# The opening of an attention stage: constant rows filled by GpSimd, and the first head's loads issued from GpSimd's queue

## The chip, the cores and the metric

The kernel runs on one core of a Trainium2 chip. A core has five engines that work in parallel, each through its own list of instructions in order: TensorE (matmuls, PE in the profile), VectorE (DVE), ScalarE (ACT), GpSimd (POOL) and SyncE (SP), which here only issues DMAs. The metric is the time of one execution on the device, in microseconds; lower is better. The time before is the median of three runs, 2979.34 us (2972.79 to 2981.46).

## What is computed

One layer of a hybrid encoder over 2064 positions (16 meta tokens and 2048 inputs) of width 1024. An input projection feeds three groups of heads side by side: an RG-LRU recurrence, a forgetting attention with 8 heads of 64, and an RWKV-7 recurrence. Their outputs go through one output projection, and a gated feed-forward block follows. The attention, cut to its core:

```python
qh = heads(q) * (HEAD_DIM ** -0.5)
kh, vh = heads(k), heads(v)
c = jnp.cumsum(log_sigmoid(f_logit + f_bias), axis=1)     # per head
s = jnp.einsum('bhqd,bhkd->bhqk', qb, kh) + (cb[..., :, None] - c[..., None, :])
s = jnp.where(kpos[None, :] <= qpos[:, None], s, -jnp.inf)
p = jax.nn.softmax(s, axis=-1)
o = jnp.einsum('bhqk,bhkd->bhqd', p, vh)
```

So each score is a product of a query and a key plus a difference of two cumulated gates.

## The kernel before, in words

The program has stages. First the input projection, in three parts over the positions, which writes queries, keys and values to scratch in HBM: `scr["qh"]` and `scr["ql"]` hold a query's high and low part, `kh` and `kl` those of a key, `ch` and `cl` those of the cumulated gate. Beside it run the two recurrences, block by block; their last blocks are still under way when the attention begins. Then come the attention, the output projection, and the feed-forward block in two halves.

The attention (class `Attn`) goes over two halves; in each it goes over the 8 heads, and per head over two steps `b` of 512 queries. In the first half a head has 1040 keys (`KHALF`), in the second 2064. A step has two parts. `maxima` computes the scores of a step once, in pieces into `mx` (L581), and reduces each to a row maximum on VectorE (L586). `weights` computes the scores again, transposed, into `sc` (L710 with `k1` and `q1`, L711 with `k2` and `q2`), takes the exponential on ScalarE and multiplies by the values into `po` (L733). The maxima run up to two steps ahead of the weights (`AHEAD`), so three sets of query tiles are in a ring.

The sums need constant rows. Of each tile, the partitions 0 to 63 hold data and the partitions 64 to 127 hold constants or rows that are added to the product:

- `q3` (queries for the maxima, three of them): zeros, then ones in two rows. `fixed` writes them with three memsets on VectorE, over 64 partitions (L496), three (L497) and one (L498), of 512 columns each.
- `q2` (queries for the second product, three of them): zeros, one memset on VectorE (L478). Row 64 is written later, with the negated maximum.
- `k2` (keys, two tiles in the first half): row 64 is one, the rest zero, written by four VectorE copies of a broadcast column of the identity (L504) of 520 columns each. Rows 65 and 66 are then overwritten by loads of `ch` and `cl` (L544, L545). Each tile holds two heads: heads 0 and 1 use the first, heads 2 and 3 the second.

`k1` holds the key's high and low part and has no constants. `keys` issues a head's five loads (L542 to L547), `maxima` the four loads of a step's queries (L568 to L571): `q3`, `q1` twice, `q2`. All are issued from SyncE, in the same list as the recurrences' small loads and stores (L1236 among them).

The order of instructions on each engine isn't the order of the source. A planner goes through the whole program with its own estimates and lists an instruction once what it needs is there, so instructions of the recurrences and of the attention stand mixed in the lists of all engines, up to about 1090 us. Attention's tiles lie on memory of the input projection, and the first of its instructions stand in each list behind the input projection's last ones.

GpSimd's work in the attention is the causal mask at the diagonal (L717), most of the sums of weights (L754) and part of the divisions. Before it, it does small steps of the recurrences (L1222, L1233, L1244). DMAs from its queue occur at two places, the zero columns at the program's start (L2204) and the last attention step's division (L781 to L804).

Of the kernel before, what the change touches and what calls it, by code (L numbers as in the profile page):

```python
# [8 lines left out]
F32 = mybir.dt.float32  # L9
# [23 lines left out]
class Core:  # L33


    def __init__(self, tc, ctx):
        self.tc = tc
        self.nc = tc.nc
        self.ctx = ctx
        self.uid = 0  # L40
        nc = self.nc
        self.const = ctx.enter_context(tc.tile_pool(name="const", bufs=1))
        self.ident = self.const.tile([P, P], F32, name="ident")
        make_identity(nc, self.ident[:])
        self.flip = 0
        self.root = self.apart = False
        self.turns = 0
# [319 lines left out]
KHALF = META + 8 * P  # L367
# [85 lines left out]
class Attn:  # L453
# [7 lines left out]
    def __init__(self, core, pool, psum, more, scr):  # L461
        self.core, self.pool, self.psum, self.more, self.scr = core, pool, psum, more, scr
        self.wide, self.bank, self.place, self.tail = False, 0, 0, False
        nc = self.nc = core.nc
        self.clock, self.later, self.serial, self.added = 0, [], 0, 0
        self.pending, self.loads, self.steps, self.beside = None, [], [], iter(())
        self.marks = {}
        self.place_p = 0


        self.turn = {"k": 1, "k2": 1, "q2": 0, "q3": 0}
        self.ring = {s: [] for s in self.turn}
        for i in range(self.AHEAD + 1):
            q3 = pool.tile([P, 512], F32R, tag=f"q3_{i}", name=core.n("q3"), bufs=1)
            self.fixed(q3, None, self.ONES)
            self.ring["q3"].append(q3)
            q2 = pool.tile([P, 512], F32R, tag=f"q2_{i}", name=core.n("q2"), bufs=1)
            nc.vector.memset(q2[64:128].bitcast(F32), 0.0)  # L478
            self.ring["q2"].append(q2)
            if i > 1:  # L480
                continue
            k1 = pool.tile([P, 2, KHALF], F32R, tag=f"k1_{i}", name=core.n("k1"), bufs=1)
            self.rear(pool, f"k2_{i}")
            v1 = pool.tile([P, 2, NKT // 2 + 1, 64], F32, tag=f"v1_{i}", name=core.n("v1"), bufs=1)
            self.ring["k"].append((k1, v1))

    def rear(self, pool, tag):
        k2 = pool.tile([P, 2, KHALF], F32R, tag=tag, name=self.core.n("k2"), bufs=1)
        self.fixed(None, k2, self.ONES)
        self.ring["k2"].append(k2)  # L490

    def fixed(self, q, k, ones):

        if q is not None:

            self.nc.vector.memset(q[64:128].bitcast(F32), 0.0)  # L496
            self.nc.vector.memset(q[64 : 64 + ones + 2].bitcast(F32), 1.0)  # L497
            self.nc.vector.memset(q[64 : 64 + ones].bitcast(F32), 0.0)  # L498
        if k is not None:
            if ones == 1:  # L500
                col = self.core.ident[64:128, 64:65]
                kf = k.rearrange("p h t -> p (h t)")
                for c in range(0, 2 * KHALF, KHALF // 2):
                    self.nc.vector.tensor_copy(kf[64:128, c : c + KHALF // 2], col.to_broadcast([64, KHALF // 2]))  # L504
            else:
                self.nc.gpsimd.memset(k[64:128].bitcast(F32), 0.0)
                self.nc.gpsimd.memset(k[64 : 64 + ones].bitcast(F32), 1.0)
# [18 lines left out]
    def keys(self, h, nt):  # L526

        nc, scr = self.nc, self.scr
        n = META + P * (nt - 1)
        r = slice(64 * h, 64 * h + 64)  # L530
        if n <= KHALF:

            i, half = divmod(self.place, 2)
            self.place = (self.place + 1) % 4
            k1, v1 = (t[:, half] for t in self.ring["k"][i])
            k2 = self.ring["k2"][i][:, half]
        else:
            (k1, v1), k2 = self.next("k"), self.next("k2")
            k1, k2 = (t[:].rearrange("p h t -> p (h t)") for t in (k1, k2))
            v1 = v1[:].rearrange("p h j d -> p (h j) d")  # L540
        k1f, k2f = k1.bitcast(F32), k2.bitcast(F32)
        nc.sync.dma_start(k2f[0:64, :n], scr["kh"][r, :n])  # L542
        g = 64 + self.ONES
        nc.sync.dma_start(k2f[g : g + 1, :n], scr["ch"][h : h + 1, :n])  # L544
        nc.sync.dma_start(k2f[g + 1 : g + 2, :n], scr["cl"][h : h + 1, :n])  # L545
        nc.sync.dma_start(k1f[0:64, :n], scr["kh"][r, :n])
        nc.sync.dma_start(k1f[64:128, :n], scr["kl"][r, :n])  # L547

        def values():
            nc.sync.dma_start(v1[:, : nt - 1], scr["v"][: n - META, r].rearrange("(j p) d -> p j d", p=P))  # L550
            nc.sync.dma_start(v1[:META, nt - 1], scr["v"][n - META : n, r])


        self.loads.append(values)
        return k1, k2, v1

    def maxima(self, h, b, keys):

        nc, core, scr = self.nc, self.core, self.scr
        k1, k2, v1 = keys  # L560
        r = slice(64 * h, 64 * h + 64)
        t0, n, ref = META + 512 * b, 512, 4 * b
        qt = [(P * i, P, META + P * (4 * b + i)) for i in range(4)]
        ts = slice(t0, t0 + n)
        q3 = self.next("q3")
        q1 = self.t([P, 512], "q1", F32R, self.AHEAD + 1)
        q2 = self.next("q2")
        nc.sync.dma_start(q3[0:64, :n].bitcast(F32), scr["qh"][r, ts])  # L568
        nc.sync.dma_start(q1[0:64, :n].bitcast(F32), scr["qh"][r, ts])
        nc.sync.dma_start(q1[64:128, :n].bitcast(F32), scr["qh"][r, ts])  # L570
        nc.sync.dma_start(q2[0:64, :n].bitcast(F32), scr["ql"][r, ts])  # L571
        nq = len(qt)
        mc = self.t([P, 4, 5], "mc")
        nc.vector.memset(mc[:], NEG)
        for i, (qo, rows, prior) in enumerate(qt):
            for ci in range(len(MAX_CUTS) - 1):
                a, e = MAX_CUTS[ci], min(MAX_CUTS[ci + 1], prior + rows)
                if a >= e:
                    break
                ps, last = self.mx(), e == prior + rows  # L580
                nc.tensor.matmul(ps[:rows, : e - a], q3[:, qo : qo + rows], k2[:, a:e], start=True, stop=not last)  # L581
                if last:
                    nc.tensor.matmul(
                        ps[:rows, prior - a : e - a], core.identb[:], core.futureb[:], start=False, stop=True
                    )
                self.reduced = nc.vector.tensor_reduce(  # L586
                    mc[:rows, i, ci : ci + 1], ps[:rows, : e - a], axis=AX.X, op=ALU.max
                )
                yield None
        bias = self.t([P, NKT], "bias", bufs=self.AHEAD + 1)  # L590
        yield q1, q2, bias
        sh = self.t([P, 4], "sh")
        nc.vector.tensor_reduce(sh[:], mc[:], axis=AX.X, op=ALU.max)
        ps = self.mx()
        for i in range(nq):
            nc.tensor.transpose(ps[0:1, P * i : P * i + P], sh[:, i : i + 1], core.ident[:])
        nc.scalar.activation(q2[64:65], ps[0:1], AF.Identity, scale=-1.0, bias=core.ncref[:, ref, h : h + 1])
        nc.scalar.activation(
            bias[:], core.ccol[:, :, h], AF.Identity, scale=-1.0, bias=core.cref[:, ref, h : h + 1]
        )  # L600
        yield None
# [70 lines left out]
    def pieces(b):  # L672

        ends = [META + P * (4 * b + i + 1) for i in range(4)]
        return sum(sum(a < e for a in MAX_CUTS[:-1]) for e in ends)

    def weights(self, h, b, keys, queries, fill):


# [1766 lines left out]
```

## Time and profile before

| | |
|---|---|
| median of three runs | 2979.34 us |
| the profiled execution, its own time | 2974.88 us |
| span of the profile, first to last instruction | 2973.2 us |
| mean granted TensorE clock | 0.980 |
| first attention load issued by SyncE (L542) | 869.60 us |
| first attention matmul (L710) | 877.62 us |
| last transposed scores (L711) | 1515.5 us |
| DMA share of GpSimd's queue (q0) | 0.93 MB of 530.52 MB |

A row of the profile gives line, engine, operation, the tile written and the tiles read, and the number of instructions; buffer numbers are left out of the names, so `q1`, `q2` and `q3` all appear as `q`, `k1` and `k2` as `k`. Arrows in brackets name what ended an engine's wait. The granted clock is the share of TensorE's full rate that the chip allowed in a stretch.

### The profile page before, as it was taken

How to read it: one execution, taken by the hardware profiler on the slowest of the kernel's cores; microseconds unless marked ns; L12 is line 12 of the kernel's file. 1: busy time of each engine (PE TensorE's matmuls, PEld its weight loads, DVE VectorE, ACT ScalarE, POOL GpSimd, SP SyncE). 2: the span in 40 equal slices, each digit the busy share in tenths (PEclk: the TensorE clock that was granted, in tenths of full speed). 3: DMA queues.
4: the chain of work that ended last, by engine and by line, in shares of the span. 5: the costliest groups of instructions: out<-in, count | busy, mean ns of one | idle time of the engine just before them, and what ended most of it. 6: DMA issues, size and time to landing. Idle time of an engine off the chain costs nothing.

```text
span 2973.2 us, 53343 instructions
## 1 busy us (share of the span) xinstructions
PE 2840.2 (96%) x18854; PEld 2448.6 (82%) x18854; DVE 2015.4 (68%) x3974; ACT 1505.3 (51%) x2937; POOL 1281.3 (43%) x1555
## 2 busy tenths in 40 slices
PE   6999999999978889999999999999999999999998
PEld 6998899889865555566568999999999999787887
DVE  5257654675678766556756988888778787646766
ACT  4246432444346555445635665666575665324333
POOL 1001121131214566766722667455655444656443
PEclk9999899999989899999999999999999999999999
DMA  6776479576654257535245665577777774436453
GB/s 219 235 233 223 156 246 322 171 240 213 209 127 95 70 130 215 125 95 130 72 133 187 204 191 173 167 230 211 205 212 219 218 199 131 155 114 222 148 171 121
DMA packets 470344, 530.52 MB, mean 178 GB/s; under 512 B 86862, under 2 KB 356888, under 8 KB 468524
## 3 DMA queue, kind: packets, MB, share of 16 engines
q1 hardware_dynamic: 469308, 526.18, 58.4%
q8 instruction: 148, 2.42, 0.3%
q14 instruction: 120, 0.98, 0.1%
q0 software_dynamic: 768, 0.93, 0.1%
HBM read 368.07 MB, written 158.90 MB: 177 GB/s over the span
## 4 chain that ended last, share of the span: by engine, by line
PE 72%; DVE 8%; DMA 7%; ACT 5%; POOL 4%; issue 3%; SPq 1%; DVEq 0%; POOLq 0%; ACTq 0%
PE psu L181 9%; PE psu L182 9%; PE psu L183 9%; PE psp L183 5%; PE psp L182 5%; PE psp L181 5%; PE psd L181 4%; PE psd L182 4%; PE psd L183 4%; PE po L733 3%; PE sc L710 2%; PE pswo L181 2%; PE pswo L182 2%; PE pswo L183 2%; PE mx L581 2%
## 5 line engine op out<-in xcount | busy, mean ns | idle before, releaser
L182 PE MATMUL psu<-xo,uw 128*128 128x344 f32 x1848 | 591.5, 320 | 0.0
L181 PE MATMUL psu<-xo,uw 128*128 128x344 f32 x1848 | 586.0, 322 | 3.5 <-DVE vb L1907 2.1
L183 PE MATMUL psu<-xo,uw 128*128 128x344 f32 x1848 | 581.9, 320 | 0.3 <-DVE uw L1716 0.3
L181 PE MATMUL psp<-xh,wh 128*128 128x384 f32 (+2 forms) x1152 | 378.3, 328 | 0.1
L183 PE MATMUL psp<-xh,wl 128*128 128x384 f32 (+2 forms) x1152 | 377.0, 328 | 0.7 <-DMA wl<-scr_wk 0.7
L182 PE MATMUL psp<-xl,wh 128*128 128x384 f32 (+2 forms) x1152 | 377.6, 328 | 0.0
L1716 DVE TENSOR_TENSOR uw<-uq,uw 128x512 fp32r<-128x512 f32 x341 | 318.8, 940 | 61.3 <-ACT uw L1715 58.3
L181 PEld LDWEIGHTS psu<-xo,uw 128*128 128x128 f32 x1848 | 345.8, 188 | 5.1 <-DVE vb L1907 3.1
L182 PEld LDWEIGHTS psu<-xo,uw 128*128 128x128 f32 x1848 | 347.2, 188 | 0.0
L183 PEld LDWEIGHTS psu<-xo,uw 128*128 128x128 f32 x1848 | 345.7, 188 | 1.1 <-DVE uw L1716 1.1
L1715 ACT ACTIVATE uw<-uq 128x512 fp32r<-128x512 f32 x462 | 288.1, 627 | 100.1 <-PE psu L183 47.3
L715 ACT ACTIVATE p<-sc,bias 128x512 f32<-128x512 f32 (+4 forms) x352 | 196.4, 590 | 166.8 <-PE sc L711 141.9
L586 DVE TENSOR_REDUCE mc<-mx 128x1 f32<-128x512 f32 (+5 forms) x352 | 191.8, 566 | 119.4 <-PE mx L581 82.9
L1855 DVE SCALAR_TENSOR_TENSOR uy<-psu,ffn_cols,uy 128x342 f32<-128x342 f32 (+1 forms) x390 | 220.6, 567 | 62.4 <-ACT uy L1853 60.7
L1716 POOL TENSOR_TENSOR uw<-uq,uw 128x512 fp32r<-128x512 f32 x121 | 184.1, 1521 | 136.7 <-ACT uw L1715 112.9
L1863 POOL TENSOR_TENSOR uy<-uy,uy 128x342 f32<-128x342 f32 (+1 forms) x132 | 144.2, 1092 | 228.7 <-DVE uy L1855 63.1
L183 PEld LDWEIGHTS psp<-xh,wl 128*128 128x128 f32 x1152 | 219.9, 191 | 7.1 <-issue 4.6
L181 PEld LDWEIGHTS psp<-xh,wh 128*128 128x128 f32 x1152 | 219.8, 191 | 4.5 <-issue 2.6
L182 PEld LDWEIGHTS psp<-xl,wh 128*128 128x128 f32 x1152 | 220.0, 191 | 3.7 <-issue 2.3
L754 POOL TENSOR_TENSOR acc<-acc,p 128x512 f32<-128x512 f32 (+3 forms) x186 | 196.5, 1059 | 48.5 <-DVE acc L754 21.4
L1716 DVE TENSOR_TENSOR fo<-u,fo 128x896 fp32r<-128x896 f32 x88 | 100.3, 1140 | 133.0 <-ACT fo L1715 132.4
L1715 ACT ACTIVATE fo<-u 128x896 fp32r<-128x896 f32 x88 | 81.2, 923 | 207.6 <-PE psd L183 122.3
(489 smaller groups left out, 6301.5 us busy)
## 6 DMA issues: line engine op xcount, KB each, us to landing
uq<-scr_us SPq DMA_DIRECT2D x220, 256.0 KB
uq<-in_ffn_up_dram SPq DMA_DIRECT2D x209, 256.0 KB
wl<-scr_wk SPq DMA_DIRECT2D x48, 512.0 KB
wh<-scr_wk SPq DMA_DIRECT2D x48, 512.0 KB
u<-scr_ff SPq DMA_DIRECT2D x88, 256.0 KB
scr_ff<-uy SPq DMA_DIRECT2D x110, 171.0 KB
raw<-in_w_in_dram SPq DMA_DIRECT2D x24, 512.0 KB
scr_wk<-wh SPq DMA_DIRECT2D x24, 512.0 KB
```

The source lines that it names most:

```text
L181: nc.tensor.matmul(out, ah, bh, start=first, stop=False, skip_group_check=more)
L182: nc.tensor.matmul(out, ah, bl, start=False, stop=False, skip_group_check=more)
L183: nc.tensor.matmul(out, al, bh, start=False, stop=last, skip_group_check=more)
L581: nc.tensor.matmul(ps[:rows, : e - a], q3[:, qo : qo + rows], k2[:, a:e], start=True, stop=not last)
L586: self.reduced = nc.vector.tensor_reduce(mc[:rows, i, ci : ci + 1], ps[:rows, : e - a], axis=AX.X, op=ALU.max)
L715: last = nc.scalar.activation(p[:rows, :w], ps[:rows, :w], AF.Exp, bias=bias[:rows, j : j + 1])
L733: mm = nc.tensor.matmul(po[at : at + 64, c0:n], v1[:rows, j], p[:rows, : n - c0], start=start and i < 2, stop=end and i + 2 >= len(group), ...
L754: eng.tensor_tensor(a, ps_[0][0][:rows, c0:n] if start and i == 1 else a, p[:rows, : n - c0], op=ALU.add)
L1715: core.nc.scalar.activation(hi, src, AF.Copy)
L1716: (eng or core.nc.vector).tensor_tensor(lo, src, hi, op=ALU.subtract)
L1855: core.conved = stt(y[:, :n], src[:, i : n + i], cw[:, 44 * i + cc : 44 * i + cc + 1], y[:, :n], op0=ALU.mult, op1=ALU.add)
L1863: core.pooled = nc.gpsimd.tensor_tensor(v[:, :n], g[:, :n], v[:, :n], op=ALU.mult)
```

## The change

Three edits. The constants of the six query tiles are written by memsets on GpSimd. The second key tile's constants are written by two GpSimd memsets over all its 2080 columns, 64 partitions and then one, in place of four VectorE copies; the first key tile stays on VectorE. And for the first head in the first half, the loads of `k2` (three) and the query loads of its two steps (eight) are issued from GpSimd instead of SyncE; the two loads of `k1` stay on SyncE.

```diff
         for i in range(self.AHEAD + 1):
             q3 = pool.tile([P, 512], F32R, tag=f"q3_{i}", name=core.n("q3"), bufs=1)
-            self.fixed(q3, None, self.ONES)
+            self.fixed(q3, None, self.ONES, nc.gpsimd)
...
-            nc.vector.memset(q2[64:128].bitcast(F32), 0.0)
+            nc.gpsimd.memset(q2[64:128].bitcast(F32), 0.0)
...
-            self.rear(pool, f"k2_{i}")
+            self.rear(pool, f"k2_{i}", nc.gpsimd if i else None)
...
-    def fixed(self, q, k, ones):
+    def fixed(self, q, k, ones, eng=None):
         if q is not None:
-            self.nc.vector.memset(q[64:128].bitcast(F32), 0.0)
-            self.nc.vector.memset(q[64 : 64 + ones + 2].bitcast(F32), 1.0)
-            self.nc.vector.memset(q[64 : 64 + ones].bitcast(F32), 0.0)
+            eng = eng or self.nc.vector
+            eng.memset(q[64:128].bitcast(F32), 0.0)
+            eng.memset(q[64 : 64 + ones + 2].bitcast(F32), 1.0)
+            eng.memset(q[64 : 64 + ones].bitcast(F32), 0.0)
         if k is not None:
-            if ones == 1:
+            if ones == 1 and eng is None:
...
-        nc.sync.dma_start(k2f[0:64, :n], scr["kh"][r, :n])
+        queue = nc.gpsimd if h == 0 and n <= KHALF else nc.sync
+        queue.dma_start(k2f[0:64, :n], scr["kh"][r, :n])
         g = 64 + self.ONES
-        nc.sync.dma_start(k2f[g : g + 1, :n], scr["ch"][h : h + 1, :n])
-        nc.sync.dma_start(k2f[g + 1 : g + 2, :n], scr["cl"][h : h + 1, :n])
+        queue.dma_start(k2f[g : g + 1, :n], scr["ch"][h : h + 1, :n])
+        queue.dma_start(k2f[g + 1 : g + 2, :n], scr["cl"][h : h + 1, :n])
...
-        nc.sync.dma_start(q3[0:64, :n].bitcast(F32), scr["qh"][r, ts])
-        nc.sync.dma_start(q1[0:64, :n].bitcast(F32), scr["qh"][r, ts])
-        nc.sync.dma_start(q1[64:128, :n].bitcast(F32), scr["qh"][r, ts])
-        nc.sync.dma_start(q2[0:64, :n].bitcast(F32), scr["ql"][r, ts])
+        queue = nc.gpsimd if h == 0 and b < 2 else nc.sync
+        queue.dma_start(q3[0:64, :n].bitcast(F32), scr["qh"][r, ts])
+        queue.dma_start(q1[0:64, :n].bitcast(F32), scr["qh"][r, ts])
+        queue.dma_start(q1[64:128, :n].bitcast(F32), scr["qh"][r, ts])
+        queue.dma_start(q2[0:64, :n].bitcast(F32), scr["ql"][r, ts])
```

The other call of `fixed`, for the meta tokens in the second half, passes no engine and does what it did.

More of the change, by code (lines that the diff above doesn't have):

```diff
@@ L482, in __init__, with rear @@
             k1 = pool.tile([P, 2, KHALF], F32R, tag=f"k1_{i}", name=core.n("k1"), bufs=1)
-            self.rear(pool, f"k2_{i}")
+            self.rear(pool, f"k2_{i}", nc.gpsimd if i else None)
             v1 = pool.tile([P, 2, NKT // 2 + 1, 64], F32, tag=f"v1_{i}", name=core.n("v1"), bufs=1)
             self.ring["k"].append((k1, v1))
-    def rear(self, pool, tag):
+    def rear(self, pool, tag, eng=None):
         k2 = pool.tile([P, 2, KHALF], F32R, tag=tag, name=self.core.n("k2"), bufs=1)
-        self.fixed(None, k2, self.ONES)
+        self.fixed(None, k2, self.ONES, eng)
         self.ring["k2"].append(k2)
-    def fixed(self, q, k, ones):
+    def fixed(self, q, k, ones, eng=None):
         if q is not None:
-            self.nc.vector.memset(q[64:128].bitcast(F32), 0.0)
-            self.nc.vector.memset(q[64 : 64 + ones + 2].bitcast(F32), 1.0)
-            self.nc.vector.memset(q[64 : 64 + ones].bitcast(F32), 0.0)
+            eng = eng or self.nc.vector
+            eng.memset(q[64:128].bitcast(F32), 0.0)
+            eng.memset(q[64 : 64 + ones + 2].bitcast(F32), 1.0)
+            eng.memset(q[64 : 64 + ones].bitcast(F32), 0.0)
         if k is not None:
-            if ones == 1:
+            if ones == 1 and eng is None:
                 col = self.core.ident[64:128, 64:65]
```

## The prediction

> **What bounds the kernel now.** I read the page first: its busy times say that TensorE is the bound over the whole program. The change touches only the opening of the attention, so the whole-program shares say little; I went to the timelines of TensorE, VectorE, GpSimd and SyncE around 870 us, then to the table of stretches with the granted clock.
>
> ```profile
> PE 2840.2 (96%) x18854; PEld 2448.6 (82%) x18854; DVE 2015.4 (68%) x3974; ACT 1505.3 (51%) x2937; POOL 1281.3 (43%) x1555
> ```
> Columns of a timeline: start, length, engine, line, operation, and in brackets the idle time before it and what ended it. First TensorE at the seam between the input projection and the attention:
> ```profile
> 871.39 0.69 PE L1384 MATMUL rps<-rww,rwsc 128*64 128x64 f32 x16
> 877.62 1.10 PE L710 MATMUL sc<-q,k 128*128 128x512 f32 x2 [5.54 <-DMA q<-scr_qh]
> 883.73 0.49 PE L581 MATMUL mx<-k,q 128*128 128x144 f32 x1 [5.01 <-DVE q L498]
> ```
> The engine that is busy 96% of the program stands still here for 5.54 and 5.01 us, 10.5 us in all. The first gap ends with a load of queries, the second with a VectorE memset of a constant query row: just the two things that the change moves. This is what VectorE does meanwhile:
> ```profile
> 871.47 0.48 DVE L496 MEMSET q<- 64x512 f32 x1
> 872.51 1.46 DVE L504 CAST k<-ident 64x520 fp32r<-64x520 f32 x4
> 874.95 1.40 DVE L504 CAST k<-ident 64x520 fp32r<-64x520 f32 x4
> 877.97 0.42 DVE L1389 TENSOR_REDUCE rwgsm<-rps 128x4 f32<-128x256 f32 x1
> 883.19 1.03 DVE L498 MEMSET q<- 1x512 f32 x2 [0.16 <-DVE rwgsm L1390]
> ```
> It works without a pause: constants, and between them the recurrences' last block. GpSimd has nothing to do from 864.2 to 892.3 us, and SyncE gets to the attention's first load only at 869.6, behind the eight small loads of the recurrences:
> ```profile
> 863.88 0.31 POOL L1233 MEMSET rwxu<- 128x256 f32 x1 [4.69 <-PE rps L1328]
> 892.27 0.28 POOL L717 TENSOR_SCALAR_AFFINE_SELECT p<-p 128x112 f32<-128x112 f32 x1 [28.08 <-ACT p L715]
> 864.21 4.39 SPq L1236 DMA_DIRECT2D rwxu<-dx  x8
> 869.60 0.47 SPq L542 DMA_DIRECT2D k<-scr_kh  x1
> 873.31 0.26 SPq L544 DMA_DIRECT2D k<-scr_ch  x1
> 874.40 0.59 SPq L570 DMA_DIRECT2D q<-scr_qh  x1
> ```
> The clock makes the gap dearer than it looks (columns: stretch, its length, busy time of PE, PEld, DVE, ACT, POOL, granted clock, DMA share, GB/s):
> ```profile
> 875.00:876.00 1.00, 0.00 (x0) 0.00 (x0) 1.00 (x5) 0.00 (x0) 0.00 (x0) 1.00 0.74 176
> 876.00:877.00 1.00, 0.00 (x0) 0.00 (x0) 0.89 (x4) 0.00 (x0) 0.00 (x0) 0.52 0.73 207
> 884.00:890.00 6.00, 4.05 (x14) 2.28 (x14) 5.43 (x23) 1.45 (x3) 0.00 (x0) 0.50 1.20 221
> 890.00:900.00 10.00, 9.84 (x52) 7.48 (x52) 7.41 (x18) 4.50 (x11) 4.60 (x10) 0.67 1.06 216
> 896.00:897.00 1.00, 1.00 (x6) 0.52 (x6) 0.56 (x2) 0.65 (x3) 0.89 (x2) 0.74 1.06 216
> 897.00:898.00 1.00, 1.00 (x8) 0.70 (x7) 1.00 (x3) 0.54 (x4) 0.19 (x1) 1.00 1.00 200
> ```
> The clock falls to half at 876, about 3.9 us after TensorE's last matmul ended (872.1), and is whole again from about 896.4. From 884 to there TensorE is busy some 4.05 + 6.3 = 10.3 us at half rate; at the full rate the same matmuls would take about 5.2 us less.
>
> **The change, part by part.**
>
> *Off VectorE.* Twelve memsets (three query tiles, three for `q3` and one for `q2` each) and four of the eight casts, those of the second key tile:
> ```profile
> L496 DVE MEMSET q<- 64x512 f32 x3 | 1.5, 485 | 0.3
> L478 DVE MEMSET q<- 64x512 f32 x3 | 1.5, 485 | 0.2
> L497 DVE MEMSET q<- 3x512 f32 x3 | 1.5, 485 | 0.2 <-DVE rwrav L1134 0.2
> L498 DVE MEMSET q<- 1x512 f32 x3 | 1.5, 485 | 0.3 <-DVE rwgsm L1390 0.2
> ```
> 12 x 0.485 = 5.8 us plus 1.4 us of casts: 7.2 us. VectorE then holds only the first key tile's casts (871.5 to about 873), so the recurrences' L1389 can come near 873 instead of 878. That chain is not what TensorE waits for at the seam, so I book nothing for it alone.
>
> *Onto GpSimd.* The same twelve memsets, two memsets of 64x2080 in place of the four casts, and eleven issues of loads. The rows that price them lie far from here:
> ```profile
> 0.81 0.20 POOL masks.py:197 MEMSET ident<- 128x128 f32 x1 [0.29 <-POOLq L2432]
> 2.41 4.29 POOL L2204 DMA_DIRECT2D scr_p<-zeros  x8
> 9.55 1.60 POOL L2204 DMA_DIRECT2D scr_p<-zeros  x3 [2.86 <-DMA scr_p<-zeros]
> scr_p<-zeros POOLq DMA_DIRECT2D x12, 32.0 KB, 6.3
> rb<-scr_rden POOLq DMA_DIRECT2D x2, 128.0 KB, 2.9
> ```
> 128 columns take 0.20 us and 256 columns 0.31 (L1233 above): 0.11 us more for 128 columns, so 512 columns are some 0.53 us and 2080 some 1.9. This gives 12 x 0.53 = 6.4 us and 2 x 1.9 = 3.8 us. An issue is 4.29 / 8 = 0.54 us, eleven are 5.9 us. In all 16 us, in a hole of 28 us (864.2 to 892.3): the hole covers it, and without that cover it would stand in front of the first masks (L717). A load issued by GpSimd lands after 2.9 us where two of 128 KB are seen and after 6.3 us where twelve follow each other. I take 2.9, since the query loads are of that size and kind, and keep 6.3 for the range. The row with the 2.86 us shows the tenth of the twelve waiting for an earlier one of the same queue; should the ninth to eleventh here do so, only the second step's queries are late, and their matmuls come after those of the first step.
>
> *The waits that move.* The loads of the key tile's two rows `ch` and `cl` must still follow the VectorE casts. Today SyncE stands at L544 for them; afterwards GpSimd stands there instead, with the query loads behind it at worst. The casts end at about 872.9, before GpSimd has come that far by the sum below, so I price this at nothing; if GpSimd came early it would cost the difference, at most 872.9 less its arrival. SyncE keeps the `k1` loads and gets to the second head's keys up to 11 x 0.6 us earlier. The second key tile is first filled for the third head:
> ```profile
> 888.39 0.59 SPq L542 DMA_DIRECT2D k<-scr_kh  x1
> ```
> so its constants, done well before 880, are in time.
>
> *The sum.* The decisive chain is now GpSimd's. With memsets first, as they come in the program: 864.2 + 6.4 + 3.8 = 874.4; then the loads of `kh`, `ch`, `cl` and the first `q3`, 4 x 0.54 = 2.2, gives 876.6; landing 2.9 later, 879.5. The first matmul of the maxima moves from 883.7 to 879.5: 4.2 us earlier, and the first scores' `q1` (issued by 877.7, landed by 880.6) come about as late as that, so I take 4. TensorE still stands still for over 7 us, so the clock still falls and the 10 us at half rate stay. If the loads land in 6.3 us the gain is 0.8; if the planner lets the loads go ahead of the memsets of later tiles, the key rows bind: casts at 872.9, `ch` and `cl` issued by 874 and landed near 877, gain 6.7. Does it reach the end? In the stretch behind, TensorE is the fuller engine, and later there is no room at all:
> ```profile
> 1000.00:1200.00 200.00, 178.91 (x1167) 107.76 (x1166) 131.25 (x327) 108.87 (x220) 133.93 (x186) 0.93 0.57 148
> 1200.00:1400.00 200.00, 196.54 (x909) 128.70 (x909) 113.37 (x248) 101.11 (x185) 131.93 (x191) 1.00 0.44 110
> ```
> From 1200 us on TensorE is busy 196.54 of 200, so an earlier arrival there is an earlier end. Sum: 4 us off the span.
>
> *A rule that speaks against it.* The only copies on VectorE in GpSimd's new time are the four casts that stay, 1.46 us. The Trainium skill, page "SBUF — State Buffer", section on the two physical sides of the memory, warns that a VectorE copy in its two-port mode locks GpSimd out, so that it cannot write descriptors for its own DMAs. By that rule the casts hold GpSimd up by an estimated 1.5 us at most and the gain would be 2.5 us instead of 4; no row of this profile shows it either way, and the sum goes without it.
>
> *Against the runs.* The profiled execution took 2974.88 us, 1.7 more than its span of 2973.2, and lies 4.5 below the median of 2979.34, in runs that spread over 8.7 us. The sum makes 2974.88 into 2970.9; for a median I take the same 4 us off 2979.34 and predict 2975.
>
> **The rivals.**
>
> *More than the sum.* GpSimd's loads go ahead early, VectorE's part of the recurrences closes up too, and most of the 10.5 us of standing still goes; if what is left is shorter than the 3.9 us after which the clock fell, the 5.2 us of half rate go as well. That gives 9 to 16 us, 2963 to 2970. For it: both gaps are ended by moved work. Against it: the queue and the cast keep the keys incomplete until about 877.
>
> *It does not do what it says.* The planner placed the one-row memsets (L498) last on VectorE, long after the first ones; if it does so on GpSimd, with `ch` and `cl` behind them, 864.2 + 16 + 2.9 makes 883, as now. Time unchanged: 2979.
>
> *Slower.* Attention and the recurrences' last blocks are put in one order per engine by a planner, and a changed opening gives a new order up to about 1100 us. There TensorE already has holes that bring the clock down:
> ```profile
> 970.00:980.00 10.00, 6.92 (x30) 4.12 (x31) 8.77 (x27) 3.07 (x6) 4.40 (x8) 0.83 0.56 110
> 1110.00:1120.00 10.00, 6.40 (x32) 3.53 (x29) 8.20 (x19) 2.76 (x6) 6.97 (x12) 0.75 0.66 174
> ```
> One more such hole costs what the opening shows: 3.9 us of standing still and some 5.2 us of half rate, 9 us. One of them leaves 5 us more than before, which cannot be told from no change; from the second on it decides: 4 off, 18 on, 2993. For it: VectorE is the fuller engine in those rows. Against it: VectorE gets 7.2 us of room.
>
> A smaller one: the moved loads share the DMA engines with SyncE's, whose share is 1.06 to 1.20 from 884 on; they would land nearer 6.3 us. The Trainium skill, page "DMA: Bandwidth & Descriptors", section on issuing engines, says the same: other queues save only issue time. That is the 0.8 us end of the sum.
>
> **How the numbers follow.** The sum as worked out (gain of 1 to 8 us) 0.42; more than the sum 0.30; not doing what it says 0.13; slower 0.15. About 0.3%, 9 us, is what a measurement of this kernel can tell from no change. So faster by that is 0.30, within it 0.42 + 0.13 = 0.55, slower 0.15. The range goes from the far end of the first rival, 2963, to 2987, which takes in one more hole of the clock with the runs' own spread and leaves out most of the slower case. The likeliest case alone spans 2971 to 2978.
>
> **What would show it.** In the changed profile GpSimd is busy with memsets and issues from about 864 to 880, VectorE has only four casts at the opening, and L1389 comes near 873. The first maxima matmul stands near 879.5 on a wait for a load from GpSimd's queue or for a GpSimd memset. PEclk is still 0.5 behind it for some 12 us. The stretch of 1000 to 1200 us has a TensorE busy time near 179. The prediction is wrong if GpSimd's memsets of 512 columns take much more than 0.53 us, if the planner moves GpSimd's part behind another wait, or if the new order changes the holes up to 1140 us.

## The result and the profile after

The changed kernel takes 3006.83 us (median of four runs, 3005.43 to 3010.22), the kernel before 2976.07 us (four runs, 2972.38 to 2981.46). The ratio is 1.0097, with an interval of 1.0085 to 1.0109: some 30 us slower. The profiled execution took 3010.22 us, 1.7 more than its span of 3008.5. Code behind the edit stands three lines lower: L581, L710 and L1404 of before are now L584, L713 and L1407.

TensorE's timeline at the opening of the attention (start, length, line, tiles, and in brackets the idle time before it and what ended it):

```profile
872.88 0.69 PE L1387 MATMUL rps<-rww,rwsc 128*64 128x64 f32 x16
890.12 0.66 PE L1407 MATMUL rps<-ident,rww 128*128 128x128 f32 x2 [16.55 <-DVE rww L1400]
...
891.82 1.11 PE L713 MATMUL sc<-q,k 128*128 128x512 f32 x2
...
896.31 1.09 PE L1175 MATMUL rps<-rwrav,rwbk 64*64 64x128 f32 x16
...
900.50 0.33 PE L584 MATMUL mx<-k,q 128*128 128x144 f32 x1
```

Before, TensorE stood still for 5.54 and 5.01 us, each time for an operand of the attention. Now it stands still once ahead of its first attention matmul, for 16.55 us, and not for the attention: the next instruction in its list is a transpose of the recurrence (L1407). In the kernel before that transpose stood behind the first step's maxima. Behind it now come more pieces of the recurrence (L1170 and L1175, twice), and only then the first maxima matmul. To compare traces I count from the end of the recurrences' last matmul before the gap (872.88 + 0.69 = 873.57 here, 871.39 + 0.69 = 872.08 before), since what lies ahead of it moves by a few microseconds from execution to execution. The first maxima matmul comes 900.50 - 873.57 = 26.9 us after that end; before, 883.73 - 872.08 = 11.65. It is 15.3 us late.

What the transposes wait for, on the queues and engines of that chain (SPq is SyncE's issue of a load):

```profile
877.67 0.39 SPq L1044 DMA_DIRECT2D rwraw<-scr_p  x1
...
886.69 0.35 ACT L1054 ACTIVATE rwwa<-rwraw,rwkv_om 128x64 f32<-128x64 f32 x1 [7.27 <-DMA rwraw<-scr_p]
...
880.18 0.17 DVE L1397 TENSOR_SCALAR rwgsm<-rwgsm 128x8 f32<-128x8 f32 x1
...
887.08 0.28 DVE L1055 SCALAR_TENSOR_TENSOR rwwa<-rwraw,rwkv_cols,rwwa 128x64 f32<-128x64 f32 x1 [6.73 <-ACT rwwa L1054]
...
889.28 0.69 DVE L1400 TENSOR_TENSOR rww<-rww,rwgsm 128x512 f32<-128x512 f32 x1
```

VectorE is early, as forecast: at 880.18 it has nearly finished the normalization that the transposes need. But its list has L1055 of the next block in between, which needs a raw load that was issued at 877.67 and is used at 886.69. VectorE waits 6.73 us for it, L1400 comes at 889.28, and TensorE behind that.

GpSimd's own part went as it was priced:

```profile
865.56 0.52 POOL L497 MEMSET q<- 64x512 f32 x1
...
867.43 1.83 POOL L507 MEMSET k<- 64x2080 f32 x1
...
870.14 0.58 POOL L544 DMA_DIRECT2D k<-scr_kh  x1
...
872.74 0.62 POOL L574 DMA_DIRECT2D q<-scr_ql  x1
873.35 0.70 POOL L571 DMA_DIRECT2D q<-scr_qh  x1
...
875.50 0.50 POOL L547 DMA_DIRECT2D k<-scr_cl  x1
...
879.27 0.98 POOL L499 MEMSET q<- 1x512 f32 x2
```

The landing did not. The list of DMA issues between 866 and 905 us (count, KB each, median us from issue to landing):

```profile
q<-scr_qh POOLq DMA_DIRECT2D x6, 128.0 KB, 7.5
q<-scr_ql POOLq DMA_DIRECT2D x2, 128.0 KB, 8.0
k<-scr_ch POOLq DMA_DIRECT2D x1, 4.1 KB, 8.6
k<-scr_cl POOLq DMA_DIRECT2D x1, 4.1 KB, 8.2
```

The loss has a second part. This is one stretch later in the attention, first before, then after (stretch, length, busy time of PE, PEld, DVE, ACT and POOL, granted clock, DMA share, GB/s):

```profile
1120.00:1260.00 140.00, 133.77 (x636) 79.17 (x635) 81.16 (x168) 72.43 (x134) 97.28 (x123) 0.97 0.65 175
```
```profile
1120.00:1260.00 140.00, 121.08 (x549) 68.33 (x546) 67.77 (x143) 60.53 (x111) 86.07 (x106) 0.91 0.57 152
```

TensorE stands still for 18.9 us of these 140 instead of 6.2, and the granted clock is 0.91 instead of 0.97. TensorE's longest wait there:

```profile
1128.54 0.59 PE L713 MATMUL sc<-q,k 128*128 128x272 f32 x1 [5.73 <-ACT p L718]
```

By its trace the changed kernel ends 3008.5 - 2973.2 - 1.5 (the shift ahead of the opening) = 33.8 us later: 15.3 in the opening, 18.5 behind it.

### The profile page after: what moved, and what is told of

Read it like the earlier page. It is cut to its first block, busy times and chain, and to the rows that moved or that the text cites. A ratio compares the mean times of both kernels' runs of the same rounds, so it can differ in the third digit from the quotient of the medians.

```text
span 3008.5 us, 53337 instructions
## 1 busy us (share of the span) xinstructions
PE 2852.4 (95%) x18854; PEld 2452.5 (82%) x18854; DVE 2008.9 (67%) x3958; ACT 1507.7 (50%) x2937; POOL 1304.0 (43%) x1580
## 4 chain that ended last, share of the span: by engine, by line
PE 74%; DMA 7%; DVE 7%; ACT 4%; POOL 3%; issue 3%; SPq 1%; DVEq 0%; POOLq 0%; ACTq 0%
PE psu L181 9%; PE psu L182 9%; PE psu L183 9%; PE psp L183 5%; PE psp L182 5%; PE psp L181 5%; PE psd L181 4%; PE psd L182 4%; PE psd L183 4%; PE po L736 3%; PE sc L713 2%; PE pswo L181 2%; PE pswo L182 2%; PE pswo L183 2%; PE mx L584 2%
## 5 line engine op out<-in xcount | busy, mean ns | idle before, releaser
L757 POOL TENSOR_TENSOR acc<-acc,p 128x512 f32<-128x512 f32 (+3 forms) x186 | 198.0, 1069 | 53.8 <-ACT p L718 26.9
```

Of the source, the lines that this page charges most:

```text
L757: eng.tensor_tensor(a, ps_[0][0][:rows, c0:n] if start and i == 1 else a, p[:rows, : n - c0], op=ALU.add)
```

## The experiments

**Theory.** The changed kernel is slow because the planner put TensorE's list in another order; the work on GpSimd is the occasion for it, not the cost. **Rivals.** GpSimd's memsets and its in-order queue; loads that land late, since two queues now share the DMA engines; a planner that scatters the time at every edit.

What each engine's list looks like can be read from the built kernel. TensorE's has 14105 rows. Up to row 3956 the changed kernel's is that of before; from there to row 6050 they differ at 195 places, and behind that at four single ones. (The last of the 195 begins near row 5800; the expectations below have that number.) The experiments are told apart by two things: whether the opening is in the old order, and how soon the list comes back to the old one.

**e1_rows, e2_loads: half of the change each.** In e1 both queue choices are `nc.sync` again; in e2 the constants are VectorE's again:

```diff
-        queue = nc.gpsimd if h == 0 and n <= KHALF else nc.sync
+        queue = nc.sync
...
-            self.fixed(q3, None, self.ONES, nc.gpsimd)
+            self.fixed(q3, None, self.ONES)
```

> The constant rows by GpSimd as in the changed kernel, every load back on SyncE. In its instruction list TensorE has attention's first scores and five maxima matmuls ahead of the recurrence's transposes (L1407), as before the change. Theory (the loss comes from TensorE's new order, which needs both halves of the change): no transposes are waited for, the first maxima matmul starts near 880 us instead of 883.7, no 16 us stall on L1407, 2976 us less 0 to 8: 2968 to 2979. Rival 1 (GpSimd's memsets, or what queues behind them on GpSimd, cost the time): most of the 31 us is here, 2995 to 3010. Rival 2 (two queues overfill the DMA engines and loads land late): none of it is here, 2976. Rival 3 (any new order of the planner scatters the time by tens of us): anything from 2950 to 3010.

> The eleven loads through GpSimd's queue as in the changed kernel, the constant rows back on VectorE. TensorE's list has attention's first matmuls ahead of L1407 again. Theory (order): the first maxima matmul waits for VectorE's last memset as before, near 884 us, or for a load that lands 8 us after its issue, if that is later; 2970 to 2984. Rival 1 (GpSimd's memsets): 2976. Rival 2 (loads land late because both queues share the DMA engines): most of the loss is here, 2995 to 3010, the recurrence's raw load landing some 9 us after its issue as in the changed kernel. Rival 3 (any new order scatters): anything from 2950 to 3010.

Measured: e1 2972.16 us, ratio 0.9989 (0.9975 to 1.0004); e2 2983.22, ratio 1.0012 (0.9999 to 1.0025). Neither half carries the loss; both keep attention's first matmuls ahead of the transposes. So neither GpSimd's memsets alone nor eleven loads through its queue alone cost 30 us. In e1 the mechanism that the prediction counted on is seen, TensorE's timeline:

```profile
871.81 0.69 PE L1387 MATMUL rps<-rww,rwsc 128*64 128x64 f32 x16
879.26 1.10 PE L713 MATMUL sc<-q,k 128*128 128x512 f32 x2 [6.77 <-DMA q<-scr_qh]
880.16 0.32 PE L584 MATMUL mx<-k,q 128*128 128x144 f32 x1
```

The wait for VectorE's memset is gone, and the first maxima matmul comes 7.7 us after the recurrences' end, 4.0 us earlier than before; the span is 3.7 us shorter, counted the same way.

**e5_first_set: all the loads, a third of the query constants.**

```diff
-            self.fixed(q3, None, self.ONES, nc.gpsimd)
+            self.fixed(q3, None, self.ONES, nc.gpsimd if i < 1 else None)
...
-            self.rear(pool, f"k2_{i}", nc.gpsimd if i else None)
+            self.rear(pool, f"k2_{i}")
```

> All eleven loads through GpSimd's queue and the constant rows of the first set of queries by GpSimd (4 memsets); the other two sets and the second key tile are filled by VectorE. TensorE's list has the first score and the first four maxima matmuls ahead of L1407. Theory (order): the opening is on time, the first maxima matmul between 879 and 884 us, 2968 to 2982. Rival 2 (late loads, all eleven are still on GpSimd's queue): 2995 to 3010. Rival 1 (GpSimd's memsets, of which a third is left): some 2985. Rival 3 (scatter): anything from 2950 to 3010.

Measured: 2980.45 us, ratio 0.9998 (0.9981 to 1.0015). All eleven loads go through GpSimd's queue and the loss is absent, as long as TensorE's opening keeps its order. The loads are not free there, though. GpSimd issues them from 866.18 us on in e5, beside the recurrences' small loads, and VectorE then waits 5.41 us for a DMA ahead of the recurrences' last step, and TensorE 4.74 us behind it. First before, then e5:

```profile
870.11 0.45 DVE L1240 STREAM_TRANSPOSE rwxu<-rwxu 128x256 f32<-128x256 f32 x1 [1.19 <-DMA rwxu<-dx]
870.78 0.68 PE L1379 MATMUL rps<-rstate,rwrav 64*64 64x64 f32 x16 [0.52 <-DVE rstate L1352]
```
```profile
875.32 0.45 DVE L1243 STREAM_TRANSPOSE rwxu<-rwxu 128x256 f32<-128x256 f32 x1 [5.41 <-DMA scr_qh<-sth]
875.99 1.12 PE L1382 MATMUL rps<-rstate,rwrav 64*64 64x64 f32 x16 [4.74 <-DVE rstate L1355]
```

In e2 the same two waits are 4.40 and 3.73 us; in the changed kernel, whose loads go out only from 870.14 on, VectorE's is 1.36. So in e2 and e5 the first maxima matmul comes 2 to 3 us later than before, not earlier. And e1, e2 and e5 all have lists that differ from the old one in 48 to 85 places behind row 3956, yet stay within 0.2% of it: not every new order scatters the time. Why the planner takes the costly order only for the whole change is not shown, and the whole change with the old order forced on it was not run.

**e4_order_only: the order alone, first try.** The kernel before, with two `issue_after` (an order in the list, no wait):

```diff
+                with core.tc.issue_after(core.squared[7].ins) if first else nullcontext():
                     nc.tensor.matmul(
                         ps[:rows, : e - a], q3[:, qo : qo + rows], k2[:, a:e], start=True, stop=not last
                     )
...
+                    with core.tc.issue_after(core.turned[6, 1, 1].ins) if (h, b, j) == (0, 0, 0) else nullcontext():
```

`squared[b]` is the last square product of block `b`, `turned[b, p, q]` a transpose at its end.

> The kernel before, every constant on VectorE and every load on SyncE, and one thing changed: on TensorE the first score matmul is queued behind the last transposes of the recurrence's block and the first maxima matmul behind the next block's last square (L1175 of the changed kernel), which is the order that the changed kernel has. Theory: this alone brings the loss, the first maxima matmul near 900 us instead of 883.7, and the time 16 to 31 us longer, 2992 to 3007. Rivals 1 and 2 (GpSimd's work, late loads): none of it, 2976 within 5. If the opening is late by 16 us and the end by the same, the further 15 us that the changed kernel loses between 1170 and 1230 us are another thing than the late opening.

Measured: 3016.42 us, ratio 1.0126 (1.0102 to 1.0150), 38 us slower with nothing on GpSimd. It overshot: I had taken the transposes of the block after the right one, so that the first scores came much later than in the changed kernel.

**e6_order_again: the order alone, mended** (`turned[5, 1, 1]`). TensorE's list now differs from the changed kernel's at 18 places, all between rows 3900 and 4100, and is the same row for row behind them.

> The kernel before, constants on VectorE and loads on SyncE, with TensorE's opening put in the changed kernel's order more closely than in e4_order_only (the first score matmul behind one block's transposes, the first maxima matmul behind the next block's squares). TensorE's list is now the changed kernel's nearly row for row, and differs from that of before up to the same place, row 5800 of 14105. Theory (the order alone makes the loss): first maxima matmul near 900 us, a stall of some 16 us ahead of the transposes, 3000 to 3012. Rivals that blame GpSimd's work or the loads: 2976.

Measured: 3007.58 us, ratio 1.0090 (1.0065 to 1.0115), against 1.0097 for the changed kernel. Its TensorE:

```profile
870.98 1.12 PE L1392 MATMUL rps<-rww,rwsc 128*64 128x64 f32 x16
...
888.82 0.66 PE L1412 MATMUL rps<-ident,rww 128*128 128x128 f32 x2 [16.72 <-DVE rww L1405]
...
900.71 0.68 PE L584 MATMUL mx<-k,q 128*128 128x144 f32 x1
```

Nearly the same time of standing still, 16.72 us, and the same late maxima, without one memset or load of the opening on GpSimd. The order makes the loss. The two lines fix TensorE's order alone, but the planner then writes the lists of all engines anew: VectorE's differs from that of before at 165 places and ScalarE's at 149, and from the changed kernel's at only 41 and 16. So what e6 shows is the cost of the plan that goes with this order, all lists together. What the transposes wait for is another thing here (VectorE still has the constants to write) and ends at the same time.

**e8_gate_late: the changed kernel, less of the stall.** One VectorE instruction moved in its list:

```diff
-            nc.vector.scalar_tensor_tensor(out, v(raw[:, p, :n]), k["mu"][:, cc], out, op0=ALU.mult, op1=ALU.add)
+            with self.core.tc.issue_after(self.core.normeds[5].ins) if (row, c0, p) == (768, PAD + self.start(8), 0) else nullcontext():
+                nc.vector.scalar_tensor_tensor(out, v(raw[:, p, :n]), k["mu"][:, cc], out, op0=ALU.mult, op1=ALU.add)
```

`normeds[b]` is L1400 of block `b`.

> The changed kernel with one VectorE instruction (L1055, the next block's gate input, which waits for the recurrence's raw load that lands 9 us after its issue) queued behind L1400, on which TensorE's first transposes wait. All of GpSimd's work and loads stay. TensorE's opening keeps the changed kernel's order; its list is that of before again from row 4690 on. Theory: L1400 ends near 883 instead of 890 us, the stall on L1407 falls from 16.6 to some 10 us, first maxima matmul near 894 us, and with the later list back the loss is some 10 us, 2982 to 2992. Rival (the late loads themselves hold the opening, not VectorE's order): stall unchanged, 3000 to 3010. Rival (a late opening costs the late arrival and 15 us more): 2997 to 3003.

Measured: 2994.14 us, ratio 1.0049 (1.0032 to 1.0065). The stall is what the chain above says it should be:

```profile
868.23 0.69 PE L1389 MATMUL rps<-rww,rwsc 128*64 128x64 f32 x16
878.59 0.66 PE L1410 MATMUL rps<-ident,rww 128*128 128x128 f32 x2 [9.67 <-DVE rww L1402]
...
882.77 0.69 PE L1410 MATMUL rps<-ident,rww 128*128 128x128 f32 x2 [2.67 <-ACT rww L1417]
```

So VectorE's wait for the late raw load was 6.9 us of the 16.55. But a wait of 2.67 us stands ahead of the next transposes, and the first maxima matmul is still 11.4 us late instead of 15.3. Half of the loss is gone, yet the list came back to the old one at row 4700 as well; the count of score matmuls below puts nearly all of the gain, in this trace, behind the opening, where the list differs. It lands 2 us above the range forecast.

**e7_rows_order, e9_behind_block, e10_maxima_behind, e11_behind_half: how late, and which list behind.** These ask whether the second part of the loss follows from a late opening or from the list that stays other. e7 is e1 with the two lines of e6. e10 is the kernel before with the first of them only. e9 puts both matmuls behind `turned[5, 1, 1]`, e11 behind `turned[5, 0, 1]`, one half block earlier.

> e1_rows (constants by GpSimd, loads on SyncE) with the same opening forced on TensorE as in e6_order_again. Here the planner's list comes back to that of the kernel before at row 4690, not at 5800. Theory in two parts (a late opening costs what it is late, 10 to 16 us, and the list that stays other up to row 5800 costs the further 15): first maxima matmul between 892 and 900 us, and the end only as late as that, 2984 to 2994. Rival (a late opening costs 31 us whatever the list is afterwards): 3000 to 3010. Rival (the loads through GpSimd are needed for the loss): 2972.

> The kernel before with a milder order: the first score and the first maxima matmul both behind one block's transposes, but ahead of the next block's squares. The opening is late by some 8 us (transposes near 889, first maxima matmul near 891), and the list differs from that of before up to row 6050. Theory in two parts: 8 us of the opening and about 15 of the later list, 2995 to 3005. Rival (only the lateness of the opening counts): 2982 to 2988. Rival (the opening doesn't reach the end): 2976.

> The kernel before with one thing forced: the first maxima matmul behind the next block's squares, as in the changed kernel; the first score stays early. The opening is as late as in e6_order_again (first maxima matmul near 899 us, 16 late), but the planner's list comes back to that of the kernel before at row 4690. Theory in two parts (lateness, and the list that stays other up to row 5800): 13 to 18 us over the kernel before, 2990 to 2996. Rival (the lateness alone brings 30 us): 3003 to 3011. Rival (list alone): 2976.

> The kernel before with the first score and the first maxima matmul behind the first half of one block's transposes: first maxima matmul near 890 us, 7 late, almost as in e9_behind_block, but the list is that of the kernel before again from row 4660 on (e9_behind_block: from 6050). Theory in two parts: 5 to 10 us, 2982 to 2988. Rival (the lateness costs twice what it is, as e9_behind_block's 17 us for 8.4 could be read): 2992 to 2997.

Measured: e7 2997.16 us, ratio 1.0063 (1.0041 to 1.0085); e9 2996.21, 1.0057 (1.0040 to 1.0075); e10 3002.16, 1.0092 (1.0074 to 1.0110); e11 2981.99, 1.0020 (1.0009 to 1.0032). The cleanest pair is e9 and e11, whose edits differ by one index. TensorE's timeline of e9 and then of e11:

```profile
872.15 0.69 PE L1392 MATMUL rps<-rww,rwsc 128*64 128x64 f32 x16
...
892.13 0.47 PE L584 MATMUL mx<-k,q 128*128 128x144 f32 x1
```
```profile
872.45 1.12 PE L1392 MATMUL rps<-rww,rwsc 128*64 128x64 f32 x16
...
891.38 0.68 PE L584 MATMUL mx<-k,q 128*128 128x144 f32 x1
```

and the later stretch of e9 and then of e11:

```profile
1120.00:1260.00 140.00, 124.67 (x579) 71.42 (x576) 77.61 (x163) 65.42 (x120) 87.81 (x112) 0.94 0.60 159
```
```profile
1120.00:1260.00 140.00, 130.39 (x615) 76.15 (x615) 82.52 (x174) 71.14 (x131) 93.72 (x116) 0.94 0.65 173
```

The openings are late by 7.6 and 6.2 us, nearly the same; e11's list is the old one again by row 4700, e9's only at 6050, as the changed kernel's; and e9 loses 17 us and e11 six, in intervals that don't overlap. e7 lies 3 us above its forecast, e9 inside and e11 at the lower end. In the later stretch e9's TensorE is busy 124.67 us, e11's 130.39. Where the later list costs its time can be read without any shift: from the 219th of the 704 score matmuls (`sc`, in order of their start), by which TensorE's list is the old one again in the eight kernels of the table with 4700, to the last. First before, then the changed kernel:

```profile
1128.52 0.29 PE L710 MATMUL sc<-q,k 128*128 128x272 f32 x1
...
1515.53 0.17 PE L711 MATMUL sc<-q,k 128*16 128x16 f32 x1
```
```profile
1147.62 0.39 PE L713 MATMUL sc<-q,k 128*128 128x272 f32 x1
...
1549.99 0.17 PE L714 MATMUL sc<-q,k 128*16 128x16 f32 x1
```

This takes 387.0 us before and 402.4 in the changed kernel, 15.4 more. All kernels side by side, each counted in its own trace (lateness of the first maxima matmul and of the end of the span, less the shift ahead of the opening as above; then what the stretch from the 219th to the last score matmul takes more than before). In e2 and e5 a wait stands ahead of the recurrences' last matmuls, so these two are counted from the start of the group ahead of it (869.58 in the kernel before, 869.37 and 870.57 there):

| kernel | old list again by row | first maxima matmul, us | end of span, us | 219th to last score matmul, us more | ratio of times |
|---|---|---|---|---|---|
| e12 (below) | 4700 | -5.5 | -5.3 | -0.1 | 0.9979 |
| e1 | 4700 | -4.0 | -3.7 | +5.1 | 0.9989 |
| e5 | 4700 | +2.0 | +4.3 | -1.4 | 0.9998 |
| e2 | 4700 | +3.2 | +2.2 | -0.4 | 1.0012 |
| e11 | 4700 | +6.2 | +9.7 | +3.1 | 1.0020 |
| e8 | 4700 | +11.4 | +18.0 | +0.4 | 1.0049 |
| e7 | 4700 | +14.8 | +23.1 | +4.2 | 1.0063 |
| e10 | 4700 | +21.3 | +20.4 | +1.6 | 1.0092 |
| e9 | 6050 | +7.6 | +22.0 | +16.6 | 1.0057 |
| changed kernel | 6050 | +15.3 | +33.8 | +15.4 | 1.0097 |
| e6 | 6050 | +17.0 | +20.9 | +12.9 | 1.0090 |
| e4 | 6080 | +20.4 | +41.4 | +11.3 | 1.0126 |

Where the list comes back, the end is as late as the opening, give or take -1 to +8 us. Where it doesn't, 14 to 21 us are added in three of four, and 3.9 in e6, whose profiled execution is the shortest of its four runs (2995.86 us against a median of 3007.58). The stretch of score matmuls parts the kernels without an exception: 11.3 to 16.6 us more where the list stays other, -1.4 to 5.1 where it comes back. e6 has its 12.9 there too; what it lacks, it won back ahead of the 219th. And e8 ends 15.8 us ahead of the changed kernel, 15.0 of them in this stretch. e10 missed its forecast of 13 to 18 us and came within 1 us of its rival's 3003 (the lateness alone): its opening came out 21 us late instead of 16, in part because TensorE ran the next block's squares at a lower clock (eight of them took 2.07 us; the same eight, L1167, take 1.16 in the kernel before). So there are two parts, a late opening that passes to the end give or take 8 us, and a later list with more holes. In the changed kernel's trace they are of like size, 15.3 us in the opening and 15.4 between the 219th and the last score matmul. Each kernel was traced once, so how the parts vary between executions is open, and why the later list is worse I have not traced beyond its waits.

**e12_loads_first: the better half, and one wait less.** In e1 SyncE stands for 2 us at the key rows' load `ch`, which must follow VectorE's casts, with the first query loads behind it. e12 queues the two row loads behind the first three of these:

```diff
-        queue.dma_start(q1[64:128, :n].bitcast(F32), scr["qh"][r, ts])
+        moved = queue.dma_start(q1[64:128, :n].bitcast(F32), scr["qh"][r, ts])
+        if h == 0 and b == 0:
+            with core.tc.issue_after(moved.ins):
+                self.rows()
```

> e1_rows (constants by GpSimd, loads on SyncE) with the first head's ch and cl loads, which wait for VectorE's casts and hold SyncE for some 2 us in e1_rows (from 870.6 to 873.2), issued behind the first step's query loads. TensorE's list is the same as that of e1_rows, row for row. Theory (the opening's arrival passes to the end one to one): first score near 876.5 instead of 879.3, first maxima matmul near 877.5 instead of 880.2, 2 to 3 us under e1_rows and 5 to 8 under the kernel before: 2968 to 2972. Rival (the gain is taken back by a later wait): as e1_rows, 2972 to 2976.

Measured: 2971.14 us, ratio 0.9979 (0.9965 to 0.9992), faster than both kernels. Its TensorE:

```profile
875.52 0.69 PE L1395 MATMUL rps<-rww,rwsc 128*64 128x64 f32 x16
881.44 1.10 PE L721 MATMUL sc<-q,k 128*128 128x512 f32 x2 [5.23 <-DMA q<-scr_qh]
882.33 0.32 PE L592 MATMUL mx<-k,q 128*128 128x144 f32 x1
```

The wait for the query load is 5.23 us instead of e1's 6.77, the first maxima matmul 5.5 us earlier than in the kernel before, the end 5.3. Its lead over e1 (0.9979 against 0.9989, with intervals that overlap) is not shown.

## Why the prediction was wrong, step by step

- **GpSimd's prices: right.** Memsets of 512 columns took 0.52 us (forecast 0.53), of 2080 columns 1.83 (1.9), issues 0.50 to 0.70 (0.54), and the needed part ended at 880.25.
- **VectorE: right.** Only the four casts are left, and L1392 (L1389 of before) is at 874.37, 1.5 us of which is the shift.
- **"I take 2.9" for the landing: wrong.** The 128 KB loads landed after 7.5 and 8.0 us, worse than the far end of 6.3, and the 4 KB rows after 8.6 and 8.2. The load of `cl` was issued at 875.50 and landed near 883.7, 10.1 us after the recurrences' end instead of before's 11.65. By this landing alone the gain would have shrunk to an estimated 1.5 us of the 4. In e5 and e2, with the old order and the query loads issued earlier, the same loads landed after 4.6 to 5.0 us (128 KB) and 1.9 to 3.3 (4 KB); the opening gained nothing there either, for the waits shown under e5. The smaller rival had the mechanism: the Trainium skill, page "DMA: Bandwidth & Descriptors", section "Issuing engines are not separate DMA queues", says that DMAs from several engines run on the same DMA engines and that issuing from more of them saves only issue time. The trace agrees: the DMA share of 874 to 886 us rose from 0.80 to 1.05, and the moved bytes only from 192 to 225 GB/s:

```profile
874.00:886.00 12.00, 2.72 (x8) 1.61 (x9) 11.04 (x31) 1.23 (x3) 0.00 (x0) 0.59 0.80 192
```
```profile
874.00:886.00 12.00, 0.00 (x0) 0.00 (x0) 5.42 (x16) 0.63 (x1) 6.25 (x11) 0.51 1.05 225
```

- **"The decisive chain is now GpSimd's": the step that failed.** The sum took for granted that TensorE's next instruction after L1384 is the attention's. In the new list it is the recurrence's transpose, and L1389's chain, of which I wrote "I book nothing for it alone", became the one that TensorE waits for: 16.55 us at L1407, and a first maxima matmul 15.3 us late instead of 4 early.
- **"So an earlier arrival there is an earlier end": right** in the two traces that have one (e1 4.0 to 3.7, e12 5.5 to 5.3). A later arrival reaches the end too, with up to 8 us more where the list comes back.
- **The slower rival had the mechanism and the wrong weight.** It named a new order by the planner, but counted it in holes of 9 us from the stretch of 970 to 1120 and gave it 0.15; the first hole was at the opening itself and longer, 16.55 us, and the later list added the rest. TensorE's busy time from 1000 to 1200, forecast near 179, is 170.10:

```profile
1000.00:1200.00 200.00, 170.10 (x1036) 102.81 (x1033) 120.61 (x307) 102.13 (x206) 126.59 (x182) 0.91 0.53 137
```

- **The rule on GpSimd's lock-out** (the Trainium skill, page "SBUF — State Buffer", section "SBUF: two separate sides") would have cost an estimated 1.5 us. During the four casts (872.82 to 874.28) GpSimd's two issues took 0.62 and 0.70 us instead of 0.52: 0.3 us, far less; this trace does not show the casts holding GpSimd up for their length.

## What to carry to other kernels

Where a planner writes the engines' lists, an edit off the critical engine can move work on the critical one: compare the critical engine's list before and after, around the edit, before pricing the edit itself. Find the first instruction that each list puts next after a stall, and price what that one waits for. And test the halves of a change apart: here one half alone kept the order, and its trace shows the gain that the whole was forecast to give (3.7 us of 4), though its ratio of 0.9989 is not clear of no change.

## What the runs showed of the hardware

Loads delay each other across issuing queues. The recurrence's raw load of 65 KB was in use 2.75 us after its issue before, and 9.0 us after it in the changed kernel (877.67 to 886.69, above). In all nine kernels whose opening loads come from SyncE alone it was 1.9 to 2.8 us; in e8, with the moved loads beside it, 8.3. In the kernel before:

```profile
880.46 0.39 SPq L1041 DMA_DIRECT2D rwraw<-scr_p  x1
...
883.21 0.35 ACT L1051 ACTIVATE rwwa<-rwraw,rwkv_om 128x64 f32<-128x64 f32 x1 [10.79 <-DMA rwraw<-scr_p]
```

A load of 4 KB waited as long as one of 128 KB (8.2 to 8.6 against 7.5 to 8.0 us), and the first load that GpSimd issued there, 260 KB at 870.14, landed after 4.7. So in that stretch the time to land went by what was under way, not by the load's own size.
